# Gate splits at other ticks, decay work ordered behind retention scores, other statistics for three last tiles and a later silu table in a one-core encoder layer

## Chip, cores and metric

The kernel runs on one core of a Trainium2 chip. The metric is the device time of one execution in microseconds (us): the median of three runs of the kernel before is 1171.52 us, from 1171.24 to 1172.17.

## What is computed

One layer of an encoder on 1024 tokens of width 1024, all in float32. In the words of the reference, cut:

```python
u = x @ w_in                                        # rq rk rv rg | aq ak av
y_ret = swish(rg) * groupnorm(ret_fwd + ret_bwd)    # 8 heads of 64, chunks of 128
y_att = windowed_gqa(aq, ak, av, sink)              # 8 query heads, 2 kv heads, +-128 tokens, ALiBi
h = layer_norm(ALPHA * x + concat(y_ret, y_att) @ w_out)
ffn = (silu(h @ w_gate) * (h @ w_up)) @ w_down      # hidden 2816
ple = sigmoid(h @ w_ple_gate) * (p @ w_ple_proj)
out = layer_norm(ALPHA * h + ffn + ple)
```

Retention of one direction and one head is done in 8 chunks: `scores = q @ k.T * decay`, `y_inner = scores @ v`, `kv = (k * k_decay).T @ v` of each chunk, a scan `state = state * chunk_decay + kv` over the chunks, and `y_cross = (q * q_decay) @ state`.

## The kernel before

Every large float32 matmul is three fp32r passes: an operand is split into a high part (ScalarE copy) and a low part (VectorE subtraction, lines 71 and 72), and TensorE adds hi*hi, hi*lo and lo*hi (lines 77 to 79 in the first phase, 803 to 805 later). The products with W_out, with w_ple_gate and of the feed-forward part are made by a seven-product scheme (Strassen's), so their operands are first added or subtracted in halves.

**The order of the first phase, to about 355 us.** TensorE's order is written out by hand, as a list of steps ("ticks", some 0.9 us each). Eight heads of retention and eight of attention are done in four pairs. While one pair's retention and attention are worked on, TensorE multiplies the next pair's projections, step by step, and small pieces of the pair's own work are put between these steps. VectorE, ScalarE, SyncE (SP, which issues the DMAs) and GpSimd (POOL) get their order from a scheduler, which places their instructions beside TensorE's; `behind` is an order dependency without a semaphore that keeps an instruction behind the latest matmul of the main stream. The retention pieces of one pair are, in class `Retention`: `keys` (transposes of k into PSUM, then VectorE's multiplication by the key decay, line 411; the tiles are called `qq` for chunks 0 to 3 and `pt` for 4 to 7), `kv` (matmuls at line 428 out of both tiles, evicted by VectorE at 436 and by ScalarE at 434), `scan` (12 small instructions at 441 and 444, then four DMAs that write the states), `scores` (matmuls at 459, multiplication by the decay at 461 into `pt`, and the queries' decay at 464 into `qq`), `out` (matmuls at 478 to 481), `evict` (ScalarE squares at 488 and 489, VectorE at 490 and 491) and `norm` (matmuls with ones at 498, then 500, and 519 some ticks later). Attention's pieces are `scores` (548 and 549, with VectorE's bias and maximum at 550, `st` at 552, ScalarE's exponential at 554; some ticks later 558 and the scaling at 560), `turn` (transposes at 572, evicted at 574) and `values` (584).

**Side work.** The weight w_ple_gate is split ahead of its use: `presplit_gate` makes 28 operands. Each is one `put` (ScalarE copy at 602, VectorE subtraction at 603, one 512 KB store to DRAM tensor `pgd` by SP), 16 of them behind one VectorE sum at 663. They rotate through two buffers `pro`. The list `at` gives the tick at which each of 30 items is put out. Line 251 is the eviction of attention's queries (`aq`).

**W_out.** About 354 to 376 us VectorE makes sums and low halves of W_out's operands (lines 870, 872, 876 and 72), ScalarE the high halves (71) and evictions of the first products (972).

**Feed-forward.** From about 541 us all five engines' orders are written by hand. Units of 12 matmul passes (2.72 us each) make gate and up products; `finish` applies ScalarE's Silu in place (1388). A one-element Silu stands ahead of the units in the code (1854); the table of an activation function is loaded by an ACT_TABLE_LOAD ahead of the first instruction that needs another table.

**The end.** The last unit finishes tiles 0 to 3 of the output one after the other, 18 matmul passes each, in `tail`: add the product (`addto`, 1618 or 1620), mean and variance (`var`), reciprocal deviation (`rstd`: VectorE, then POOL's power at 1652), `center` (1657, times the gain) and `scale` (1662, plus the bias, then a 256 KB store of each half on SP). For tile 3 the statistics come from VectorE's bn_stats and bn_aggr (1622, 1641); for tiles 0 to 2 the sum comes with the addition (1618) or from ScalarE (1624), and the squares from ScalarE (1635). Tiles 4 to 7 are finished earlier by `ln2_steps`: ScalarE at 1674, VectorE at 1677, and a DMA issued from POOL that adds the bias to the tile (1678), then one 512 KB store each on SP.

Of the kernel before, what the change touches and what calls it, by code (L numbers as in the profile page):

```python
# [16 lines left out]
P = 128  # L17
# [25 lines left out]
def layer(tc, xT, xn, w_first, w_mt, w_rv, w_out, w_pg, w_pe, pT, w_gu, w_dn,  # L43
# [37 lines left out]
    def behind(ins):  # L81

        tc.add_manual_dep(ins.ins, recent[0], mybir.DependencyInfo(
            mybir.DependencyClass.NoSync, mybir.DependencyReason.DATA), reason="order")
        return ins
# [307 lines left out]
    class Retention:  # L393
# [44 lines left out]
        def scan(self):  # L438
            i, U = self.i, self.U
            for n in range(1, 7):  # L440
                dve.scalar_tensor_tensor(U[0][:, n, :], U[0][:, n - 1, :], cd[:, i:i + 1], U[0][:, n, :],
                                         ALU.mult, ALU.add)
                k = 6 - n
                dve.scalar_tensor_tensor(U[1][:, k, :], U[1][:, k + 1, :], cd[:, 4 + i:5 + i], U[1][:, k, :],
                                         ALU.mult, ALU.add)
# [4 lines left out]
        def scores(self, hh):  # L450
# [9 lines left out]
            for h in range(2):  # L460
                dve.tensor_tensor(pt[:, h], bb[h], self.dt[:, h, :].unsqueeze(1).to_broadcast([P, 4, P]), ALU.mult)
            qq = self.qq[hh] = bt([P, 2, 4, P], "qq")
            for h in range(2):
                dve.tensor_tensor(qq[:, h], dq[:, h, :].rearrange("p (n c) -> p n c", n=4),
                                  self.qd[:, h, :].unsqueeze(1).to_broadcast([P, 4, P]), ALU.mult)
# [179 lines left out]
    def presplit_gate():  # L645
# [9 lines left out]
        def steps(k):  # L655
# [21 lines left out]
        at = [2 + 3.4 * k for k in range(12)] + [55 + 2.5 * k for k in range(2)] + [65 + 1.9 * k for k in range(7)] + \  # L677
            [78.5 + 2 * k for k in range(9)]
# [935 lines left out]
    def addto(t, h, b, op=ALU.add, done=False):  # L1614


        if done and t != LAST and op == ALU.add:
            dve.tensor_tensor_reduce(half(t, h), half(t, h), b, 1.0, 0.0, op, ALU.add, stts[t][:, h:h + 1])
            return
        dve.tensor_tensor(half(t, h), half(t, h), b, op)  # L1620
        if done and t == LAST:
# [4 lines left out]
    LAST = 3  # L1626
# [10 lines left out]
    def var(t):  # L1637

        stt = stts[t]
        if t == LAST:  # L1640
# [6 lines left out]
    def rstd(t):  # L1647
        stt = stts[t]
        if t != LAST:
# [32 lines left out]
    def tail(products):  # L1682

        bs = dbank[len(SEG) - 1, GRP[4]]
        for t in range(4):
            products(t)
            if t:
                rstd(t - 1)
            addto(t, 0, bs[t], done=True)
            var(t)  # L1690
            if t < LAST:
                if t:
                    scale(t - 1)
                center(t)
        rstd(LAST)
        scale(LAST - 1)
        center(LAST)
        scale(LAST)
# [140 lines left out]
    with tc.manual_schedule(engines={ET.PE, ET.DVE, ET.Activation, ET.Pool, ET.SP}):  # L1839
# [14 lines left out]
        act.activation(fsum[3][:, 0:1], fsum[0][:, 0:1], AF.Silu)  # L1854
        ahead_g(-1, 4)
        for k in range(NG):
# [9 lines left out]
            ahead_g(k, k + 1 + min(9, 4 + k))  # L1866
            while stores and stores[0][0] <= k:
# [105 lines left out]
```

## Time and profile before

| | before |
|---|---|
| median of 3 runs | 1171.52 us |
| the profiled execution's own time | 1172.7 us |
| span of its trace | 1170.6 us |
| granted clock of TensorE | 0.998 |
| TensorE (PE) busy | 1156.5 us, 99% |
| VectorE (DVE) busy | 900.4 us, 77% |
| ScalarE (ACT) busy | 580.1 us, 50% |
| GpSimd (POOL) busy | 121.0 us, 10% |
| SP's DMA queue | 195.94 MB, 47.6% of 16 DMA engines' span |
| POOL's DMA queue | 16.78 MB, 8.2% |

A row of a timeline gives the start, the busy time, the engine, the line of the kernel, the operation, the tile written and the tiles read, their shape, a count where several alike follow one another, and in brackets the idle time before it with what ended that. Instructions of one engine overlap somewhat: one of 0.69 us can follow the last by 0.60.

### The profile page before, as it was taken

To read this page: it belongs to the slowest core of one execution; us is meant where nothing else is said; L and a number is where in the kernel's file an instruction comes from. 1 tells how busy PE (TensorE), PEld (TensorE's weight loads), DVE (VectorE), ACT (ScalarE), POOL (GpSimd) and SP (SyncE) were. 2 spreads that over 40 slices of the span, in tenths; PEclk is the share of its full clock that TensorE was granted. 3 is DMA by queue.
4 is the path that set the end of the run, shared out by engine and by line. 5 is a ranking of instruction groups with operands and counts; after the bars stand their busy time and mean duration, and the time that the engine had idled before them with its cause. 6 is when DMAs were issued, how large, how long until landed. Compare 5 with 4: busy or idle time off the path is not lost.

```text
span 1170.6 us, 17933 instructions
## 1 busy us (share of the span) xinstructions
PE 1156.5 (99%) x6330; PEld 971.5 (83%) x6330; DVE 900.4 (77%) x1746; ACT 580.1 (50%) x1181; POOL 121.0 (10%) x181
## 2 busy tenths in 40 slices
PE   9999999999999999999999999999999999999996
PEld 7888888788887888888888888888888888888885
DVE  4666688777869688947998988888888976773677
ACT  5566348686756256214445434443344445552463
POOL 2001021202010021000000000000000020133232
PEclk9999999999999999999999999999999999999999
DMA  6345665746356955665322222232223289999977
GB/s 252 100 153 207 246 207 193 244 159 223 127 190 230 365 172 196 261 195 201 117 90 105 112 105 100 102 135 101 99 72 136 89 249 349 350 225 203 261 173 216
DMA packets 84378, 213.86 MB, mean 183 GB/s; under 512 B 12225, under 2 KB 17473, under 8 KB 84289
## 3 DMA queue, kind: packets, MB, share of 16 engines
q1 hardware_dynamic: 75648, 195.94, 47.6%
q0 software_dynamic: 8640, 16.78, 8.2%
q8 instruction: 50, 0.82, 0.3%
q14 instruction: 40, 0.32, 0.1%
HBM read 141.32 MB, written 62.16 MB: 174 GB/s over the span
## 4 chain that ended last, share of the span: by engine, by line
PE 86%; DVE 6%; DMA 4%; ACT 2%; issue 1%; POOL 0%; SPq 0%; DVEq 0%; ACTq 0%; POOLq 0%
PE bmm L803 8%; PE bmm L804 8%; PE bmm L805 7%; PE bt L803 6%; PE bt L804 6%; PE bt L805 6%; PE bmm L77 4%; PE bs L803 4%; PE bs L805 4%; PE bs L804 4%; PE bmm L79 4%; PE bmm L78 4%; PE bo L805 3%; PE bo L803 3%; PE bo L804 3%
## 5 line engine op out<-in xcount | busy, mean ns | idle before, releaser
L77 PE MATMUL bmm<-H,w 128*128 128x512 f32 x240 | 97.3, 405 | 0.0
L78 PE MATMUL bmm<-H,w 128*128 128x512 f32 x240 | 93.9, 391 | 0.0
L79 PE MATMUL bmm<-H,w 128*128 128x512 f32 x240 | 93.9, 391 | 0.0
L1388 ACT ACTIVATE ev<-ev 128x512 f32<-128x512 f32 x42 | 26.5, 630 | 104.3 <-DVE ev L1417 92.8
L1562 POOL DMA_DIRECT2D h0b<-in_w_dn x24 | 21.6, 899 | 540.7 <-DVE ev L1368 504.9
L77 PEld LDWEIGHTS bmm<-H,w 128*128 128x128 f32 x240 | 45.1, 188 | 11.1 <-issue 1.4
L79 PEld LDWEIGHTS bmm<-H,w 128*128 128x128 f32 x240 | 45.1, 188 | 10.3
L78 PEld LDWEIGHTS bmm<-H,w 128*128 128x128 f32 x240 | 45.2, 188 | 7.9
L554 ACT ACTIVATE sc<-sc,st 128x385 f32<-128x385 f32 (+1 forms) x64 | 37.2, 585 | 15.6 <-DVE st L552 15.3
L550 DVE CUSTOM_DVE_ANT_0 sc<-cst,bs,skb 128x384 f32<-128x384 f32 (+1 forms) x64 | 35.0, 575 | 8.3 <-PE bs L549 7.8
L1417 DVE TENSOR_TENSOR ev<-ev,bt 128x512 f32<-128x512 f32 x44 | 30.1, 683 | 12.5 <-PE bt L805 12.5
L1368 DVE TENSOR_TENSOR ev<-ev,bs 128x256 f32<-128x256 f32 x63 | 25.6, 418 | 15.5 <-PE bs L805 14.7
L1390 DVE TENSOR_TENSOR ev<-ev 128x512 f32<-128x512 f32 x42 | 29.0, 691 | 10.5 <-ACT ev L1388 9.0
L803 PE MATMUL bmm<-H,u 128*128 128x512 f32 x92 | 36.2, 393 | 0.2 <-ACT ev L1426 0.2
L804 PE MATMUL bmm<-H,u 128*128 128x512 f32 x92 | 36.0, 392 | 0.0
L805 PE MATMUL bmm<-H,u 128*128 128x512 f32 x92 | 35.8, 389 | 0.0
L72 DVE TENSOR_TENSOR w<-raw,w 128x512 fp32r<-128x512 f32 x34 | 23.1, 688 | 16.2 <-ACT w L71 16.1
L545 POOL COPY sc<-skb 128x1 f32<-128x1 f32 x64 | 15.6, 253 | 188.9 <-PE bt L572 144.5
L560 ACT ACTIVATE sc<-sc,st 128x384 f32<-128x384 f32 (+1 forms) x64 | 34.2, 580 | 1.2 <-DVE st L558 0.9
L71 ACT ACTIVATE H<-ln 128x512 fp32r<-128x512 f32 (+1 forms) x34 | 22.7, 675 | 21.2 <-DVE ln L1052 7.2
L803 PE MATMUL bmm<-H,w 128*128 128x512 f32 x84 | 32.9, 392 | 0.0
L804 PE MATMUL bmm<-H,w 128*128 128x512 f32 x84 | 32.9, 392 | 0.0
(802 smaller groups left out, 3898.4 us busy)
## 6 DMA issues: line engine op xcount, KB each, us to landing
ad<-ev SPq DMA_DIRECT2D x33, 512.0 KB, 2.6
pgd<-pro SPq DMA_DIRECT2D x28, 512.0 KB, 3.0
raw<-in_w_gu SPq DMA_DIRECT2D x22, 512.0 KB, 3.6
ln<-in_w_gu SPq DMA_DIRECT2D x22, 512.0 KB, 3.9
raw<-ad SPq DMA_DIRECT2D x40, 256.0 KB, 5.6
ln<-ad SPq DMA_DIRECT2D x37, 256.0 KB, 6.0
H<-in_w_dn SPq DMA_DIRECT2D x33, 256.0 KB, 7.4
wod<-aq SPq DMA_DIRECT2D x15, 512.0 KB, 2.8
```

Source lines behind the costliest of these rows:

```text
L77: pe.matmul(o, lh, rh, start=start, stop=False)
L78: pe.matmul(o, lh, rl, start=False, stop=False)
L79: recent[0] = pe.matmul(o, ll, rh, start=False, stop=stop).ins.name
L550: dve.tensor_tensor_reduce(sc[g][:, :nk], cst[:, tc0:tc0 + nk], b[:, :nk], slope(i, g), skb[:, 2 * i + g:2 * i + g + 1], ALU.add, ALU.max, ...
L554: act.activation(sc[g][:, :nk + 1], sc[g][:, :nk + 1], AF.Exp, bias=st_[:, 1, j, g:g + 1], accum_out=st_[:, 2, j, g:g + 1])
L560: behind(act.activation(sc[g][:, :nk], sc[g][:, :nk], AF.Copy, scale=st_[:, 3, j, g:g + 1]))
L803: pe.matmul(o, lh, rh, start=start, stop=False, skip_group_check=True)
L804: pe.matmul(o, lh, rl, start=False, stop=False, skip_group_check=True)
L805: pe.matmul(o, ll, rh, start=False, stop=stop, skip_group_check=True)
L1388: act.activation(c[:, 0, :], c[:, 0, :], AF.Silu)
L1390: dve.tensor_tensor(c[:, 1, :], c[:, 0, :], c[:, 1, :], ALU.mult)
L1417: dve.tensor_tensor(get(name), ev[left][:, m, :], right, ALU.add)
```

## The change

Four places change. (1) The list `at`, which spreads the gate's 30 split items over ticks: the first 14 follow one another by 2.8 ticks in place of 12 by 3.4 and 2 from tick 55 by 2.5; the next 7 begin at tick 60 in place of 65, the last 9 at 73 by 1.9 in place of 78.5 by 2. (2) A new order dependency `after`, without a semaphore, puts the 12 scan instructions and the two multiplications by the queries' decay behind the second multiplication of the retention scores (`pt`) on VectorE. (3) At the end, tiles 1 and 2 get their statistics from bn_stats and bn_aggr as tile 3 does; tile 0 is scaled by one ScalarE instruction, its bias is added by a DMA from POOL, and one 512 KB store writes it; `scale` of a tile follows its `center` at once. (4) The one-element Silu moves behind the first feed-forward unit.

```diff
--- before.py
+++ after.py
@@ -81,6 +81,11 @@
     def behind(ins):
 
         tc.add_manual_dep(ins.ins, recent[0], mybir.DependencyInfo(
+            mybir.DependencyClass.NoSync, mybir.DependencyReason.DATA), reason="order")
+        return ins
+
+    def after(ins, name):
+        tc.add_manual_dep(ins.ins, name, mybir.DependencyInfo(
             mybir.DependencyClass.NoSync, mybir.DependencyReason.DATA), reason="order")
         return ins
 
@@ -438,11 +443,12 @@
         def scan(self):
             i, U = self.i, self.U
             for n in range(1, 7):
-                dve.scalar_tensor_tensor(U[0][:, n, :], U[0][:, n - 1, :], cd[:, i:i + 1], U[0][:, n, :],
-                                         ALU.mult, ALU.add)
                 k = 6 - n
-                dve.scalar_tensor_tensor(U[1][:, k, :], U[1][:, k + 1, :], cd[:, 4 + i:5 + i], U[1][:, k, :],
-                                         ALU.mult, ALU.add)
+                for x in (dve.scalar_tensor_tensor(U[0][:, n, :], U[0][:, n - 1, :], cd[:, i:i + 1], U[0][:, n, :],
+                                                   ALU.mult, ALU.add),
+                          dve.scalar_tensor_tensor(U[1][:, k, :], U[1][:, k + 1, :], cd[:, 4 + i:5 + i], U[1][:, k, :],
+                                                   ALU.mult, ALU.add)):
+                    after(x, self.tail)
             for d in range(2):
                 for h in range(2):
                     sp.dma_start(self.states[64 * d:64 * d + 64, h, 1 - d:NT - d, :], U[d][64 * h:64 * h + 64])
@@ -458,11 +464,12 @@
                     a = slice(64 * h, 64 * h + 64)
                     pe.matmul(bb[h][:, j, :], self.rk[a, c], dq[a, h, j * P:(j + 1) * P], start=True, stop=True)
             for h in range(2):
-                dve.tensor_tensor(pt[:, h], bb[h], self.dt[:, h, :].unsqueeze(1).to_broadcast([P, 4, P]), ALU.mult)
+                self.tail = dve.tensor_tensor(pt[:, h], bb[h], self.dt[:, h, :].unsqueeze(1).to_broadcast([P, 4, P]),
+                                              ALU.mult).ins.name
             qq = self.qq[hh] = bt([P, 2, 4, P], "qq")
             for h in range(2):
-                dve.tensor_tensor(qq[:, h], dq[:, h, :].rearrange("p (n c) -> p n c", n=4),
-                                  self.qd[:, h, :].unsqueeze(1).to_broadcast([P, 4, P]), ALU.mult)
+                after(dve.tensor_tensor(qq[:, h], dq[:, h, :].rearrange("p (n c) -> p n c", n=4),
+                                        self.qd[:, h, :].unsqueeze(1).to_broadcast([P, 4, P]), ALU.mult), self.tail)
 
         def half(self, hh):
             return self.y[:, hh * HF:(hh + 1) * HF]
@@ -674,8 +681,7 @@
         k0, k1, k2, k3 = map(steps, range(4))
         k1[0] = pair_of(k1[0], lambda: load(2))
         k3[0:0] = [lambda: load(3), lambda: None]
-        at = [2 + 3.4 * k for k in range(12)] + [55 + 2.5 * k for k in range(2)] + [65 + 1.9 * k for k in range(7)] + \
-            [78.5 + 2 * k for k in range(9)]
+        at = [2 + 2.8 * k for k in range(14)] + [60 + 1.9 * k for k in range(7)] + [73 + 1.9 * k for k in range(9)]
         return [(ticks[0] + t, f) for t, f in zip(at, k0 + k1 + k2 + k3, strict=True)]
 
     def pair_of(f, g):
@@ -1614,16 +1620,16 @@
     def addto(t, h, b, op=ALU.add, done=False):
 
 
-        if done and t != LAST and op == ALU.add:
+        if done and t not in BN and op == ALU.add:
             dve.tensor_tensor_reduce(half(t, h), half(t, h), b, 1.0, 0.0, op, ALU.add, stts[t][:, h:h + 1])
             return
         dve.tensor_tensor(half(t, h), half(t, h), b, op)
-        if done and t == LAST:
+        if done and t in BN:
             dve.bn_stats(stts[t][:, 6 * h:6 * h + 6], half(t, h))
         elif done:
             act.activation(ct([P, HF], "sg", 2), half(t, h), AF.Copy, accum_out=stts[t][:, h:h + 1])
 
-    LAST = 3
+    BN = (1, 2, 3)
 
     def negmean(t):
         stt = stts[t]
@@ -1637,7 +1643,7 @@
     def var(t):
 
         stt = stts[t]
-        if t == LAST:
+        if t in BN:
             dve.bn_aggr(stt[:, 12:14], stt[:, 0:12])
             dve.tensor_scalar(stt[:, 12:13], stt[:, 12:13], -1.0, None, ALU.mult)
         else:
@@ -1646,7 +1652,7 @@
 
     def rstd(t):
         stt = stts[t]
-        if t != LAST:
+        if t not in BN:
             dve.tensor_scalar(stt[:, 13:14], stt[:, 2:3], stt[:, 3:4], 1.0 / D, ALU.add, ALU.mult)
         dve.tensor_scalar(stt[:, 14:15], stt[:, 13:14], EPS, None, ALU.add)
         pool.tensor_tensor(stt[:, 15:16], stt[:, 14:15], cst[:, C_MH:C_MH + 1], ALU.pow)
@@ -1684,18 +1690,20 @@
         bs = dbank[len(SEG) - 1, GRP[4]]
         for t in range(4):
             products(t)
-            if t:
-                rstd(t - 1)
+            if t == 1:
+                rstd(0)
             addto(t, 0, bs[t], done=True)
             var(t)
-            if t < LAST:
-                if t:
-                    scale(t - 1)
-                center(t)
-        rstd(LAST)
-        scale(LAST - 1)
-        center(LAST)
-        scale(LAST)
+            if t in BN:
+                rstd(t)
+            if t == 1:
+                act.activation(accd[0], accd[0], AF.Copy, scale=stts[0][:, 15:16])
+                pool.dma_start(accd[0], ln2[1], accum_op=ALU.add)
+            center(t)
+            if t in BN:
+                scale(t)
+            if t == 1:
+                sp.dma_start(out[0], accd[0])
 
     GRP = {1: 0, 2: 0, 5: 1, 3: 1, 6: 2, 7: 2, 4: 2}
 
@@ -1851,7 +1859,6 @@
         homes.update((name, a_tile([P, 2, HF], "ev")) for name in ("spare", "s1", "u2", "c11", "u3", "c22"))
         FINE4 = len(plan(0)) + len(plan(1)) - 2
         FINES = (2, 4, 7, 9, 20, 23, 26, FINE4)
-        act.activation(fsum[3][:, 0:1], fsum[0][:, 0:1], AF.Silu)
         ahead_g(-1, 4)
         for k in range(NG):
             gunits[k][1]()
@@ -1864,6 +1871,8 @@
                     items.insert(at, x)
                     at += 1
             ahead_g(k, k + 1 + min(9, 4 + k))
+            if k == 0:
+                act.activation(fsum[3][:, 0:1], fsum[0][:, 0:1], AF.Silu)
             while stores and stores[0][0] <= k:
                 stores.pop(0)[1]()
             j = k + 1 - NG
```

TensorE's order is the same in both kernels. Three places of VectorE's order follow, in the lines of each kernel (411, 603, 663 and 251 before are 416, 610, 670 and 256 after).

VectorE at the start of pair 1, before: the last rows up to the key decay of chunks 4 to 7 (`pt` at 411), which TensorE's first kv matmuls read; `aq` is evicted out of two PSUM banks, and ScalarE has a part of each eviction.

```order
L251 SCALAR_TENSOR_TENSOR aq_466<-bmm_1470,aq_466 64x512
L603 TENSOR_TENSOR pro_1168<-pre_1165,pro_1168 128x512
L251 SCALAR_TENSOR_TENSOR aq_1548<-bmm_1470,aq_1548 64x512
L72 TENSOR_TENSOR w_1608<-raw_1606,w_1608 128x512
L500 TENSOR_SCALAR kv_1592<-bo_1516 2x512
L251 SCALAR_TENSOR_TENSOR aq_466<-bmm_1558,aq_466 64x512
L411 TENSOR_TENSOR qq_1603<-bt_1598,kd 128x512 x2
L251 SCALAR_TENSOR_TENSOR aq_1548<-bmm_1558,aq_1548 64x512
L72 TENSOR_TENSOR w_1611<-raw_1606,w_1611 128x512
L411 TENSOR_TENSOR pt_1632<-bt_1627,kd 128x512 x2
L519 SCALAR_TENSOR_TENSOR y_1162<-y_1162,gn,kv_1485 128x512
```

The same place after the change.

```order
L256 SCALAR_TENSOR_TENSOR aq_466<-bmm_1477,aq_466 64x512
L256 SCALAR_TENSOR_TENSOR aq_1560<-bmm_1477,aq_1560 64x512
L610 TENSOR_TENSOR pro_1167<-pre_1165,pro_1167 128x512
L72 TENSOR_TENSOR w_1616<-raw_1614,w_1616 128x512
L610 TENSOR_TENSOR pro_1168<-pre_1166,pro_1168 128x512
L256 SCALAR_TENSOR_TENSOR aq_466<-bmm_1566,aq_466 64x512
L507 TENSOR_SCALAR kv_1600<-bo_1528 2x512
L416 TENSOR_TENSOR qq_1611<-bt_1606,kd 128x512
L256 SCALAR_TENSOR_TENSOR aq_1560<-bmm_1566,aq_1560 64x512
L416 TENSOR_TENSOR qq_1611<-bt_1606,kd 128x512
L72 TENSOR_TENSOR w_1619<-raw_1614,w_1619 128x512
L416 TENSOR_TENSOR pt_1640<-bt_1635,kd 128x512 x2
```

Two operands of the gate (610) stand here in place of one, two instructions of 416 are parted by an eviction, and the normalization of the last pair (519 before) no longer follows the key decay directly.

VectorE at the start of pair 2, before: the rows up to the same key decay.

```order
L603 TENSOR_TENSOR pro_1168<-pre_1163,pro_1168 128x512
L663 TENSOR_TENSOR pre_1164<-pre_1164,pre_1163 128x512
L519 SCALAR_TENSOR_TENSOR y_1596<-y_1596,gn,kv_2110 128x512
L251 SCALAR_TENSOR_TENSOR aq_2236<-bmm_2242,aq_2236 64x512
L411 TENSOR_TENSOR qq_2330<-bt_2325,kd 128x512
L603 TENSOR_TENSOR pro_1167<-pre_1163,pro_1167 128x512
L251 SCALAR_TENSOR_TENSOR aq_2237<-bmm_2242,aq_2237 64x512
L411 TENSOR_TENSOR qq_2330<-bt_2325,kd 128x512
L603 TENSOR_TENSOR pro_1168<-pre_1164,pro_1168 128x512
L72 TENSOR_TENSOR w_2335<-raw_2333,w_2335 128x512
L72 TENSOR_TENSOR w_2338<-raw_2333,w_2338 128x512
L411 TENSOR_TENSOR pt_2360<-bt_2355,kd 128x512 x2
```

And after.

```order
L256 SCALAR_TENSOR_TENSOR aq_2249<-bmm_2125,aq_2249 64x512
L507 TENSOR_SCALAR kv_2288<-bo_2201 2x512
L72 TENSOR_TENSOR w_2335<-raw_2333,w_2335 128x512
L610 TENSOR_TENSOR pro_1168<-pre_1164,pro_1168 128x512
L526 SCALAR_TENSOR_TENSOR y_1604<-y_1604,gn,kv_2116 128x512
L256 SCALAR_TENSOR_TENSOR aq_2248<-bmm_2254,aq_2248 64x512
L416 TENSOR_TENSOR qq_2330<-bt_2325,kd 128x512 x2
L256 SCALAR_TENSOR_TENSOR aq_2249<-bmm_2254,aq_2249 64x512
L72 TENSOR_TENSOR w_2338<-raw_2333,w_2338 128x512
L416 TENSOR_TENSOR pt_2360<-bt_2355,kd 128x512 x2
```

Counted from the eviction of the pair's last output (490 before, 497 after) to the second multiplication into `pt`, VectorE has 23 instructions before and 18 after: five splits and sums of the gate have moved ahead of it.

VectorE at the start of W_out, before, from the last sums of line 870 to the second of line 876 (`ln`, `h0a`, `H` and `h` are operands of W_out's products).

```order
L870 TENSOR_TENSOR ln_3854<-y_1597,y_2323 128x512
L72 TENSOR_TENSOR H_3852<-ln_3853,H_3852 128x512 x2
L872 TENSOR_TENSOR ln_3854<-ln_3854,y_1596 128x512
L72 TENSOR_TENSOR H_3851<-ln_3854,H_3851 128x512
L876 TENSOR_TENSOR ln_3853<-ln_3853,y_2321 128x512
L72 TENSOR_TENSOR H_3852<-ln_3854,H_3852 128x512
L872 TENSOR_TENSOR ln_3854<-ln_3854,y_1597 128x512
L72 TENSOR_TENSOR h0a_3895<-ln_3853,h0a_3895 128x512
L72 TENSOR_TENSOR h_3897<-y_2321,h_3897 128x512
L72 TENSOR_TENSOR H_3852<-ln_3854,H_3852 128x512
L876 TENSOR_TENSOR ln_3853<-ln_3853,y_2322 128x512
```

And after (876, 878 and 882 are 870, 872 and 876 before).

```order
L878 TENSOR_TENSOR ln_3854<-ln_3854,y_1604 128x512
L876 TENSOR_TENSOR ln_3854<-y_1605,y_2323 128x512
L882 TENSOR_TENSOR ln_3853<-ln_3853,y_2321 128x512
L72 TENSOR_TENSOR H_3852<-ln_3854,H_3852 128x512
L72 TENSOR_TENSOR H_3851<-ln_3854,H_3851 128x512
L72 TENSOR_TENSOR h0a_3895<-ln_3853,h0a_3895 128x512
L878 TENSOR_TENSOR ln_3854<-ln_3854,y_1605 128x512
L72 TENSOR_TENSOR h_3897<-y_2321,h_3897 128x512
L882 TENSOR_TENSOR ln_3853<-ln_3853,y_2322 128x512
```

From the first instruction of line 870 to the second of line 876 VectorE has 20 instructions before and 19 after. On ScalarE the table load and the one-element Silu that stood in this stretch are gone; the load that stood right in front of the first Silu of line 1388 now stands earlier, between a split (1252) and an eviction (1424) of the first units. The program has 6 table loads before and 5 after.

## The prediction

> **What bounds the kernel now.** First the busy times of the page, then TensorE's waits, then the last of the stretches into which I cut the span (its second number is TensorE's busy time).
>
> ```profile
> PE 1156.5 (99%) x6330; PEld 971.5 (83%) x6330; DVE 900.4 (77%) x1746; ACT 580.1 (50%) x1181; POOL 121.0 (10%) x181
> ...
> PE bt L428 <- DVE pt L411: 2.0, 1, 2.0
> PE bs L803 <- ACT h0b L972: 0.6, 1, 0.6
> ...
> PE bt L572 <- ACT ptr L574: 0.3, 1, 0.3
> PE bmm L803 <- ACT ev L1426: 0.2, 1, 0.2
> ...
> 1162.00:1170.60 8.60, 0.00 (x0) 0.00 (x0) 5.57 (x11) 0.00 (x0) 1.22 (x2) 0.76 0.42 161
> ```
>
> TensorE is busy 1156.5 of 1170.6 us, and its order stays. So the change can gain only where TensorE stands still, 14.1 us: 8.6 of them after its last matmul, the others in waits of which one is 2 us long and the rest are under 1. What parts 1, 2 and 4 can bring is therefore small, and what they can spoil is larger: VectorE works three quarters of the time right beside TensorE.
>
> **Pair 2's start: a gain.** VectorE ahead of the long wait, and TensorE's kv matmuls in pair 1 and in pair 2:
>
> ```profile
> 228.92 0.68 DVE L603 TENSOR_TENSOR pro<-pre,pro 128x512 fp32r<-128x512 f32 x1
> 229.52 1.29 DVE L72 TENSOR_TENSOR w<-raw,w 128x512 fp32r<-128x512 f32 x2
> 230.73 1.28 DVE L411 TENSOR_TENSOR pt<-bt,kd 128x512 f32<-128x512 f32 x2
> ...
> 169.33 1.03 PE L428 MATMUL bt<-rv,qq 128*64 128x64 f32 x28
> 170.19 0.99 PE L428 MATMUL bt<-rv,pt 128*64 128x64 f32 x28
> ...
> 229.16 1.03 PE L428 MATMUL bt<-rv,qq 128*64 128x64 f32 x28
> 232.16 0.53 PE L428 MATMUL bt<-rv,pt 128*64 128x64 f32 x11 [1.97 <-DVE pt L411]
> ```
>
> The second 28 matmuls begin 0.86 us behind the first in pair 1, 3.00 behind in pair 2: 2.14 lost, as the key decay ended only at 230.73 + 1.28 = 232.01. Back to back, VectorE starts such instructions 0.60 apart (228.92, 229.52). After the change 18 instead of 23 stand from the pair's last eviction to the decay's end, which so moves 5 x 0.60 = 3.0 us ahead, to 229.0; TensorE wants it at 229.16 + 0.86 = 230.02. **-2.15**, with 1 us of slack, enough for one late instruction. Late next is nothing near: the scan, now behind the scores' `pt`, is read several ticks later.
>
> A smaller stall is that of the turn in pair 1:
>
> ```profile
> 181.17 0.39 PE L79 MATMUL bmm<-H,w 128*128 128x512 f32 x1
> 181.84 0.33 PE L572 MATMUL bt<-cst,sc 128*128 128x128 f32 x1 [0.28 <-ACT ptr L574]
> ```
>
> Passes follow one another by 0.227; here 0.67 pass. ScalarE's scaling ahead of it hangs on a VectorE reciprocal, which now has fewer scan and split instructions before it: **-0.45**, between that and 0.
>
> **Pairs 0 and 1: losses.** The splits moved ahead must stand somewhere. In pair 1 there is little room:
>
> ```profile
> 160.25 0.69 DVE L490 COPY y<-bo 128x512 f32<-128x512 f32 x1 [2.95 <-ACT pt L489]
> ...
> 168.62 1.29 DVE L411 TENSOR_TENSOR pt<-bt,kd 128x512 f32<-128x512 f32 x2
> ...
> 165.88 0.59 ACT L250 ACTIVATE aq<-bmm 64x512 fp32r<-64x512 f32 x1 [1.21 <-DVE aq L251]
> ```
>
> The decay ended at 169.91 and TensorE took it at 170.19 without a wait: slack under 0.3. Between the eviction at 160.25 and the decay's end 15 instructions stand in place of 14, one gate operand more, 0.60 to 0.72. VectorE's 2.95 us of idle time lie ahead of this stretch, so they do not cover it; and in it `aq` goes to and fro between VectorE and ScalarE (the 1.21), so a delay can count twice. The decay then ends at 170.6 to 171.3: a stall of 0.5 to 1.2, bounds 0 and 1.4. I take **+0.9**, as both engines are nearly full there. Behind it, attention's next scores need both banks that `pt` of the retention scores frees, and that stands behind a normalization, two copies and a reciprocal which waits for ScalarE's exponential: **+0.4**, bounds 0 and 1.0, nearer to the low end as only one bank is late. In pair 0 the low half of the squares gets a gate operand and a sum ahead of it:
>
> ```profile
> 149.74 0.68 DVE L491 TENSOR_TENSOR rb<-kv,kv 128x512 fp32r<-128x512 f32 x1
> ...
> 151.40 0.39 PE L498 MATMUL bo<-rb,ones 128*128 128x512 f32 x1
> ```
>
> It ended at 150.42, 1.0 ahead of TensorE. Two multiplications of `qq` go from before it, two gate instructions come, and each gate operand may wait for the store out of its buffer: **+0.2**, bounds 0 and 0.4. The pairs together: -2.15 - 0.45 + 0.9 + 0.4 + 0.2 = **-1.1**, by the bounds from -2.6 to +0.7.
>
> **W_out's start: a small gain.** ScalarE, then VectorE, at the wait for h0b:
>
> ```profile
> 362.84 1.28 ACT L1854 ACT_TABLE_LOAD   x1
> ...
> 371.90 0.63 ACT L71 ACTIVATE h0a<-ln 128x512 fp32r<-128x512 f32 x1 [1.78 <-DVE ln L876]
> 372.44 0.58 ACT L972 ACTIVATE h0b<-bs 128x512 f32<-128x512 f32 x1
> ...
> 371.19 0.68 DVE L876 TENSOR_TENSOR ln<-ln,y 128x512 f32<-128x512 f32 x1
> ```
>
> TensorE waits for the eviction at 372.44; it stands behind the split at 371.90, and that behind VectorE's 371.19, before which ScalarE idles 1.78. So the load taken out at 362.84 brings nothing by itself: ScalarE is not late there. But the scheduler has placed the second 876 one instruction sooner, 19th in place of 20th: **-0.6**, bounds -0.6 (the whole wait) and 0.
>
> **Silu's table: a small gain.** ScalarE, then TensorE:
>
> ```profile
> 549.79 1.28 ACT L1388 ACT_TABLE_LOAD   x1 [2.41 <-DVE ev L1417]
> 557.46 0.58 ACT L1426 ACTIVATE ev<-bmm 128x512 f32<-128x512 f32 x1
> ...
> 557.50 0.39 PE L805 MATMUL bmm<-H,w 128*128 128x512 f32 x1
> 558.09 0.50 PE L803 MATMUL bmm<-H,u 128*128 128x512 f32 x1 [0.20 <-ACT ev L1426]
> ```
>
> The table had been replaced before the first Silu, so it came again, 1.28 us in ScalarE's chain. Moved ahead, it lies in the 2.41 us that ScalarE idled, and the stall of 0.59 - 0.227 goes: **-0.35**, bounds -0.36 and 0. Were that cover too short, the load would delay the eviction next to it, and the price would be of the same size.
>
> **The end: about nothing.** Tile 0's and tile 1's additions, tile 3's chain, and the DMAs of the last 35 us:
>
> ```profile
> 1149.56 0.69 DVE L1618 CUSTOM_DVE_ANT_0 acc<-acc,bmm 128x512 f32<-128x512 f32 x1 [0.40 <-PE bmm L805]
> ...
> 1153.64 0.69 DVE L1618 CUSTOM_DVE_ANT_0 acc<-acc,bmm 128x512 f32<-128x512 f32 x1 [0.35 <-PE bmm L805]
> ...
> 1161.80 0.69 DVE L1620 TENSOR_TENSOR acc<-acc,bs 128x512 f32<-128x512 f32 x1 [0.18 <-PE bs L805]
> 1162.52 0.69 DVE L1622 BATCH_NORM_STATS2 stt<-acc 128x6 f32<-128x512 f32 x1
> 1163.25 0.21 DVE L1641 BATCH_NORM_AGGREGATE stt<-stt 128x2 f32<-128x12 f32 x1
> ...
> 1163.62 1.40 DVE L1662 SCALAR_TENSOR_TENSOR acc<-acc,stt,u 128x512 f32<-128x512 f32 x2
> 1164.94 1.41 DVE L1657 SCALAR_TENSOR_TENSOR acc<-acc,stt,u 128x512 f32<-128x512 f32 x2
> 1166.27 1.41 DVE L1662 SCALAR_TENSOR_TENSOR acc<-acc,stt,u 128x512 f32<-128x512 f32 x2
> ...
> acc<-u POOLq DMA_DIRECT2D x4, 512.0 KB, 4.9
> out_y<-acc SPq DMA_DIRECT2D x4, 512.0 KB, 3.6
> ```
>
> Before, tile 2's scale (1163.62, 1.32 start to start) still stands in tile 3's chain; after, each tile is finished by itself: 0.72 + 0.73 + 0.37 + 1.32 + 1.33 = 4.47 us by the starts above, while TensorE makes a tile in 1153.64 - 1149.56 = 4.08. Two more bn_stats (2 x 0.60) ahead of tile 0 meet 0.40 of idle time: tile 0 starts 0.8 late, tile 1, 3.7 behind it without its idle 0.35, at 1154.1. Then tile 2 begins at 1158.6, tile 3 at 1163.0, and the last scale ends at 1167.5 in place of 1167.68: 1.3 saved, 1.2 lost, **-0.1**, bounds -0.6 and +0.5. Tile 0 leaves by another way: scaled on ScalarE at about 1156, its bias added by a DMA that POOL issues at about 1157, behind tile 1's power; at 4.9 us it lands at 1162, and SP's store, 3.6, ends at 1165.5. Tile 2's halves, ready at 1162.3 and 1163, stand behind it on SP, then tile 3's at 1167. What this costs the last store by sharing: **+0.2**, bounds 0 and +2.
>
> **A rule against the change.** POOL's issue beside a busy VectorE:
>
> ```profile
> 1146.81 2.34 DVE L1677 TENSOR_TENSOR acc<-acc,u 128x1024 f32<-128x1024 f32 x2
> 1148.43 0.89 POOL L1678 DMA_DIRECT2D acc<-u  x1 [2.57 <-DVE acc L1677]
> ```
>
> It took 0.89 us although VectorE was at work for most of them, so VectorE's additions did not hold it up. The Trainium skill, "SBUF — State Buffer", section "SBUF: two separate sides", warns that a DMA issued from GpSimd needs its cores to write descriptors, and that some modes of VectorE lock them out; under "Who interferes with whom" it infers that two-input operations do not. The row agrees with the second. Were the issue held until VectorE is done at 1167.5, tile 0's bias would land at 1172.4 and its store end at 1176, 6.3 us after the last landing of before (about 1169.7): by the lock the sum would be near +4.5, about 1176.
>
> **Sum.** -1.1 - 0.6 - 0.35 - 0.1 + 0.2 = -1.95. The profiled execution took 1172.7 (span 1170.6, so 2.1 lie around it); its like would take 1170.7. The median of the three runs is 1171.52, 1.2 lower: **1169.5 us**. A measurement of this kernel can tell about 0.2%, 2.3 us, from no change.
>
> **Rivals.**
> - *No new stall in pairs 0 and 1*: the scheduler's order fits TensorE after all; the +1.5 falls away: -3.45, 1168.1, down to 1167.2 with the end at its low bound. For it: ScalarE and VectorE both have idle time just ahead. Against it: 0.28 of slack at 170.19. Chance 0.22.
> - *The stall only moves*: the to and fro of `aq` counts twice, and the losses stand at their bounds, 1.4 + 1.0 + 0.4, against -2.6; with W_out and Silu at half (-0.5) and the end at +0.1: about -0.2, 1171.3; own range 1170.5 to 1172.3. Chance 0.20.
> - *Slower, at the end*: tile 0's bias DMA lands late, as POOL's four of line 1678 (median 4.9) are each queued behind the last, and SP's later stores stand behind tile 0's. It decides from a landing at 1167, when tile 3's first half is ready, ten us after the issue; from there each us is one at the end. At 1169: store and halves share 3.6 us and more, the end 3 us late, sum +1 to +4, 1172.5 to 1175.5. For it: the order on SP. Against it: twice the median. Chance 0.08, the lock above included.
> - *It does not do what it says*: `pro` has two buffers, so an operand put out earlier can wait for a store, and all runs in the old times: about 1171. Chance 0.04.
>
> The forecast has 0.46; its own range is 1168.2 to 1170.6. The range of all is 1167.3 to 1172.3; outside are the slower rival and a few hundredths of the first. Faster by over 0.2%: the first rival and four tenths of the forecast, 0.40; slower, the third and a little of the second, 0.10; within, 0.50.
>
> **What would show it.** Right: no wait of the kv matmuls at 230, one of 0.5 to 1.2 at about 170; no table load at 362, and ScalarE's first Silu without one; tile 3's addition 1.0 to 1.4 behind TensorE's end, and tile 0's store landed before tile 3's. Wrong: a wait above 1.4 in pairs 0 or 1, a last scale more than 6.5 us behind TensorE's end (5.9 before), or tile 0's store issued after tile 2 is ready by more than 3 us.

## The result, and the profile after

The changed kernel takes 1173.24 us (median of 20 runs, 1170.10 to 1174.85) against 1171.15 of the kernel before in as many runs beside it (1169.81 to 1173.66): a ratio of 1.0013, 95% interval 1.0007 to 1.0019. That is about 1.5 us slower by the ratio (2.1 by the medians), where 2 us faster was forecast, and it lies above the range. The profiled execution took 1173.84, with a span of 1172.0 against 1170.6. The profiled execution of before (1172.7) was itself 1.5 us over its median, so the two spans differ by less than the medians.

TensorE's first pass of W_out starts at 357.38 in place of 354.63: up to there 2.75 us are lost. From there to the start of its last pass it takes 805.38 in place of 806.74: behind the pairs 1.36 us are gained. The loss lies in the pairs.

TensorE's waits in the changed kernel:

```profile
PE bs L555 <- DVE pt L467: 1.8, 1, 1.8
PE bo L147 <- POOL sq L144: 1.3, 1, 1.3
PE bt L809 <- ACT h0b L978: 1.1, 1, 1.1
PE bt L433 <- DVE pt L416: 0.8, 1, 0.8
PE bt L579 <- ACT ptr L581: 0.4, 1, 0.4
PE bt L809 <- DMA u<-wod: 0.2, 1, 0.2
PE bo L505 <- DVE rb L498: 0.2, 1, 0.2
```

The wait of 2.0 for the key decay is down to 0.8, and it is another one: it stands in pair 1 now. On top stands a wait that was not in the list of before: attention's scores (line 555) for the second multiplication by the retention decay (467). Pair 2's start is free, and Silu's table lies in idle time:

```profile
233.83 0.98 PE L433 MATMUL bt<-rv,qq 128*64 128x64 f32 x28
234.68 0.82 PE L433 MATMUL bt<-rv,pt 128*64 128x64 f32 x21
...
546.61 0.63 ACT L1258 ACTIVATE w<-sums 128x512 fp32r<-128x512 f32 x1 [2.36 <-DVE sums L1294]
547.26 1.28 ACT L1875 ACT_TABLE_LOAD   x1
```

The two groups of kv matmuls begin 0.85 us apart, as in pair 1 before (0.86), where before the change 3.00 lay between them. And no wait of the first feed-forward units is left.

Pair 1 tells the rest. SP's queue, then VectorE, then TensorE, in the changed kernel:

```profile
166.53 0.41 SPq L518 DMA_DIRECT2D rnd<-sn  x1
170.19 0.33 SPq L116 DMA_DIRECT2D raw<-in_w_mt  x1
170.63 1.10 SPq L522 DMA_DIRECT2D kv<-rnd  x2
...
169.45 0.68 DVE L72 TENSOR_TENSOR w<-raw,w 128x512 fp32r<-128x512 f32 x1
...
173.70 0.69 DVE L467 TENSOR_TENSOR pt<-bs,dt 128x512 f32<-128x512 f32 x1
175.99 0.75 DVE L526 SCALAR_TENSOR_TENSOR y<-y,gn,kv 128x512 f32<-128x512 f32 x1 [1.60 <-DMA kv<-rnd]
176.66 0.68 DVE L441 COPY kv<-bt 128x256 f32<-128x256 f32 x2
177.26 0.68 DVE L467 TENSOR_TENSOR pt<-bs,dt 128x512 f32<-128x512 f32 x1
...
175.88 0.34 PE L556 MATMUL bs<-kz,aq 128*128 128x384 f32 x1
178.00 0.44 PE L555 MATMUL bs<-k,aq 128*128 128x384 f32 x1 [1.78 <-DVE pt L467]
178.52 0.63 PE L77 MATMUL bmm<-H,w 128*128 128x512 f32 x1
178.95 0.63 PE L78 MATMUL bmm<-H,w 128*128 128x512 f32 x1
```

Read it from below. TensorE waits at 176 for a PSUM bank that the second `pt` at 177.26 frees. Ahead of that stands the normalization of pair 0 (526), and VectorE idles 1.60 us for its reciprocals, which two DMAs of line 522 fetch. These were issued only at 170.63, as the load ahead of them on SP (116) waits until VectorE has read the old contents of its buffer (72, done at 170.13). A wait of one engine for a buffer has held up a DMA of another chain behind it in the same queue. Behind the stall the passes follow one another by 0.43 in place of 0.227 us. The stretches show why; the column before the last two is the granted clock:

```profile
170.00:178.00 8.00, 5.46 (x81) 4.46 (x76) 5.16 (x15) 3.49 (x10) 1.63 (x1) 1.00 0.34 101
178.00:182.00 4.00, 4.00 (x11) 3.29 (x12) 3.48 (x11) 1.59 (x5) 0.24 (x1) 0.57 0.16 42
```

From 178 to 182 the clock was 0.57: 0.43 x 4 = 1.7 us more in this execution.

The same place before the change, SP's queue and TensorE's scores:

```profile
163.43 0.38 SPq L511 DMA_DIRECT2D rnd<-sn  x1
165.79 1.10 SPq L515 DMA_DIRECT2D kv<-rnd  x2
...
168.66 0.34 SPq L111 DMA_DIRECT2D raw<-in_w_mt  x1
...
174.86 0.34 PE L549 MATMUL bs<-kz,aq 128*128 128x384 f32 x1
175.03 0.36 PE L548 MATMUL bs<-k,aq 128*128 128x384 f32 x1
```

The fetch went out 2.36 us behind its store and ahead of the load, and the scores followed one another without a wait.

W_out's start, before and then in the changed kernel, and the end of the program in the changed kernel:

```profile
353.06 0.75 DVE L519 SCALAR_TENSOR_TENSOR y<-y,gn,rb 128x512 f32<-128x512 f32 x1 [1.62 <-DMA rb<-rnd]
...
353.49 0.69 DVE L730 SCALAR_TENSOR_TENSOR y<-sq,y 128x512 f32<-128x512 f32 x1
355.40 0.75 DVE L526 SCALAR_TENSOR_TENSOR y<-y,gn,rb 128x512 f32<-128x512 f32 x1 [1.21 <-DMA rb<-rnd]
356.07 3.69 DVE L72 TENSOR_TENSOR H<-y,H 128x512 fp32r<-128x512 f32 x6
...
1158.03 0.90 POOL L1701 DMA_DIRECT2D acc<-u  x1
1164.04 0.33 SPq L1706 DMA_DIRECT2D out_y<-acc  x1
...
1162.76 0.39 PE L811 MATMUL bs<-u,u 128*128 128x512 f32 x1
1164.10 0.68 DVE L1626 TENSOR_TENSOR acc<-acc,bs 128x512 f32<-128x512 f32 x1
1167.31 1.41 DVE L1668 SCALAR_TENSOR_TENSOR acc<-acc,stt,u 128x512 f32<-128x512 f32 x2
```

VectorE's full stretch at W_out begins in both kernels with a normalization that waits for a fetch; it comes 2.3 us later, while TensorE itself comes 2.75 later. The end hangs on TensorE as before: from its last pass (1162.76) to the end of the span 9.24 us, before 1170.6 - 1161.37 = 9.23.

### The profile page after: what moved, and what is told of

Read it like the earlier page. It is cut to its first block, busy times and chain, and to the rows that moved or that the text cites. A ratio compares the mean times of both kernels' runs of the same rounds, so it can differ in the third digit from the quotient of the medians.

```text
span 1172.0 us, 17919 instructions
## 1 busy us (share of the span) xinstructions
PE 1157.2 (99%) x6330; PEld 972.9 (83%) x6330; DVE 902.5 (77%) x1746; ACT 577.1 (49%) x1169; POOL 127.6 (11%) x182
## 4 chain that ended last, share of the span: by engine, by line
PE 90%; DVE 4%; DMA 2%; ACT 2%; issue 1%; SPq 0%; POOL 0%; DVEq 0%; ACTq 0%
PE bmm L809 8%; PE bmm L810 8%; PE bmm L811 8%; PE bt L809 6%; PE bt L810 6%; PE bt L811 6%; PE bmm L77 5%; PE bmm L78 5%; PE bmm L79 5%; PE bs L811 4%; PE bs L810 4%; PE bs L809 4%; PE bo L811 4%; PE bo L810 4%; PE bo L809 4%; PE bo L591 2%
## 5 line engine op out<-in xcount | busy, mean ns | idle before, releaser
L77 PE MATMUL bmm<-H,w 128*128 128x512 f32 x240 | 97.7, 407 | 0.1
L78 PE MATMUL bmm<-H,w 128*128 128x512 f32 x240 | 94.5, 394 | 0.0
L79 PE MATMUL bmm<-H,w 128*128 128x512 f32 x240 | 94.4, 393 | 0.0
L809 PE MATMUL bmm<-H,w 128*128 128x512 f32 x84 | 32.9, 392 | 0.0
L810 PE MATMUL bmm<-H,w 128*128 128x512 f32 x84 | 32.9, 392 | 0.0
L811 PE MATMUL bmm<-H,w 128*128 128x512 f32 x84 | 32.7, 389 | 0.0
```

What stands on the lines that cost most here:

```text
L77: pe.matmul(o, lh, rh, start=start, stop=False)
L78: pe.matmul(o, lh, rl, start=False, stop=False)
L79: recent[0] = pe.matmul(o, ll, rh, start=False, stop=stop).ins.name
L809: pe.matmul(o, lh, rh, start=start, stop=False, skip_group_check=True)
L810: pe.matmul(o, lh, rl, start=False, stop=False, skip_group_check=True)
L811: pe.matmul(o, ll, rh, start=False, stop=stop, skip_group_check=True)
```

## The experiments

All comparisons are with the kernel before on the same chip; intervals are 95%. Edits are against the changed kernel unless it is said otherwise. The theory to start with (A): the gate's new ticks hold up pair 0's normalization on SP. The rivals: the order dependency does it (B), or the new end (C).

**The old ticks** (parts 2, 3 and 4 stay):

```diff
-        at = [2 + 2.8 * k for k in range(14)] + [60 + 1.9 * k for k in range(7)] + [73 + 1.9 * k for k in range(9)]
+        at = [2 + 3.4 * k for k in range(12)] + [55 + 2.5 * k for k in range(2)] + [65 + 1.9 * k for k in range(7)] + \
+            [78.5 + 2 * k for k in range(9)]
```

> The changed kernel with the gate's old ticks (parts 2, 3, 4 stay). Theory A, the gate's new ticks hold up pair 0's normalization on SP, so that TensorE loses 1.9 us in attention's scores of pair 1 and some 1.7 more in a slow clock behind it: both stalls of pair 1 and the slow matmuls of 178 to 181 are gone, the wait of 2 us at pair 2's start is back (or part of it), the time is 0.5 to 1.5 us under the kernel before, about 1170. Theory B, the order dependency of part 2 puts the second multiplication by the retention decay too late: the stall at attention's second scores stays at 1 us or more and the time is over the kernel before by 1 us or more. Theory C, the new tail costs it: 1 to 1.5 us over the kernel before with no stall in pair 1.

Measured: ratio 1.0003 (0.9990 to 1.0016). No stall in pair 1; 1.4 and 0.5 us at pair 2's start, and 1.8 us at W_out. The stalls of pair 1 follow A, but the time is no gain over the kernel before.

**The new ticks alone**: the kernel before with the new list, the diff above the other way round.

> The kernel before with the gate's new ticks alone. Theory A: the stalls of pair 1 appear (about 1 us at the kv matmuls, 1.5 or more at attention's second scores) and the clock may drop behind them; pair 2's wait is smaller; 1 to 2.5 us over the kernel before. Theory B: no stall above 0.5 us at attention's second scores, and a gain of 1 us or more. Theory C: a gain as in B.

Measured: 0.9994 (0.9985 to 1.0003), where A expected a loss. TensorE's waits in pairs 1 and 2 are short:

```profile
PE bt L579 <- ACT ptr L581: 0.3, 1, 0.3
PE bs L555 <- DVE pt L467: 0.2, 1, 0.2
```

The scores' wait is 0.2 in place of 1.8, and no wait of line 433 is left, in pair 1 or 2. So A falls: the ticks alone remove pair 2's wait and bring nothing like it in pair 1. The gain of 1 us or more that B and C had is not there either: 0.7 us, not clear of zero.

**The old end** (parts 1, 2 and 4 stay):

```diff
-    BN = (1, 2, 3)
+    LAST = 3
+    BN = (3,)
...
-            if t == 1:
-                rstd(0)
+            if t:
+                rstd(t - 1)
...
-            if t in BN:
-                scale(t)
-            if t == 1:
-                sp.dma_start(out[0], accd[0])
+            if t < LAST:
+                if t:
+                    scale(t - 1)
+                center(t)
...
```

> The changed kernel with the end of before (parts 1, 2, 4 stay). Theories A and B: the pair 1 stalls as in the changed kernel, and the time from TensorE's last matmul to the end within 0.5 us of the changed kernel's 8.9, so the time within 0.6 us of the changed kernel's. Theory C: 1 us or more faster than the changed kernel.

Measured: 1.0012 (1.0002 to 1.0022), like the changed kernel. C falls: between the two ends no difference shows that is clear of the noise. The stalls of pair 1 are there as in the changed kernel (0.7 and 1.7), but in this profile the clock behind them is not down:

```profile
178.00:182.00 4.00, 4.00 (x22) 3.43 (x21) 3.95 (x16) 2.16 (x7) 0.59 (x2) 1.00 0.35 98
```

**The end and Silu's place alone**: the kernel before with parts 3 and 4.

> The kernel before with parts 3 and 4 alone (the end and Silu's table). By the sum of the prediction: Silu 0.36 gained at the 557 us stall, W_out 0 to 0.6, the end within 0.3: 0.3 to 0.9 us under the kernel before in all theories but C, which has it 0.5 us or more over.

Measured: 0.9994 (0.9984 to 1.0004), 0.7 us, in the range of the sum but not clear of zero.

What was left was the dependency, or its meeting with the ticks (A2).

**Without the dependency** (parts 1, 3 and 4):

```diff
-                    after(x, self.tail)
+                    pass
...
-                after(dve.tensor_tensor(qq[:, h], dq[:, h, :].rearrange("p (n c) -> p n c", n=4),
-                                        self.qd[:, h, :].unsqueeze(1).to_broadcast([P, 4, P]), ALU.mult), self.tail)
+                dve.tensor_tensor(qq[:, h], dq[:, h, :].rearrange("p (n c) -> p n c", n=4),
+                                  self.qd[:, h, :].unsqueeze(1).to_broadcast([P, 4, P]), ALU.mult)
```

> The changed kernel without the order dependency of part 2 (parts 1, 3, 4 stay). Theory A2: only the new ticks and the order dependency together part the two multiplications by the retention decay and put the late normalization between them; then the stalls of pair 1 stay under 0.5 us each, pair 2's wait stays away, and the time is 1 to 1.6 us under the kernel before, the sum of the gains that parts 1 and 3 with 4 showed alone (0.7 each). Rival B2: the end and the gate's ticks together cost it, whatever the order; then the time stays within 0.7 us of the changed kernel's and above the kernel before.

Measured: 0.9999 (0.9990 to 1.0007), 1.6 us under the changed kernel by the ratios, but not the 1 to 1.6 under the kernel before that A2 had. Pair 1 has no wait. The 1.1 of lines 555 and 467 is now that of pair 2, at 233.4, where the queries' decay stands ahead of `pt`:

```profile
PE bt L809 <- ACT h0b L978: 1.2, 1, 1.2
PE bs L555 <- DVE pt L467: 1.1, 1, 1.1
```

So B2 falls, and A2 holds for pair 1. Pair 2 shows what the dependency is good for.

**The normalization later**: it goes out 6 ticks later, and so stands behind both `pt` on VectorE; SP's order is unchanged.

```diff
-            later.extend((ticks[0] + at, f) for at, f in zip(LAGS, (spread, power, store, fetch, scaled)))
+            lags = LAGS[:-1] + (LAGS[-1] + (6 if (self.i, hh) == (0, 0) else 0),)
+            later.extend((ticks[0] + at, f) for at, f in zip(lags, (spread, power, store, fetch, scaled)))
```

> The changed kernel with the normalization of pair 0's first half put out 6 ticks later, so that VectorE's order has it behind both multiplications by the retention decay; SP's order is that of the changed kernel, with the load still ahead of the fetch. Theory A2 with the place on VectorE as cause: the stall at attention's second scores falls from 1.9 to under 0.3 us, the slow matmuls behind it are gone, 2 to 4 us under the changed kernel. Rival: the stall is set by the reciprocal of attention's maximum and ScalarE ahead of it; then 0.5 us or more of it stays.

Measured: 1.0004 (0.9995 to 1.0012), about 1 us under the changed kernel, where 2 to 4 were expected. The stall at the scores is gone, but half of it comes back at the turn behind, for another reader of SP's queue:

```profile
173.98 1.29 DVE L467 TENSOR_TENSOR pt<-bs,dt 128x512 f32<-128x512 f32 x2
176.81 0.69 DVE L441 COPY kv<-bt 128x256 f32<-128x256 f32 x2 [1.54 <-DMA sn<-kv]
...
179.78 0.71 PE L580 MATMUL bt<-cst,sc 128*128 128x128 f32 x4 [0.84 <-ACT kv L439]
```

The eviction of the kv matmuls needs a buffer that the next DMA on SP (`sn`) still reads, and that one stands behind the same load and fetch.

**The load behind the fetch** on SP; VectorE's order is unchanged.

```diff
-    recent = [None]
+    recent, got, nload = [None], [None], [0]
...
-        sp.dma_start(r, src)
+        x = sp.dma_start(r, src)
+        nload[0] += 1
+        if got[0] and nload[0] == 11:
+            after(x, got[0])
...
-                    sp.dma_start(r[64 * h:64 * h + 64], home[64 * h:64 * h + 64].rearrange("q e -> (q e)").partition_broadcast(64))
+                    got[0] = sp.dma_start(r[64 * h:64 * h + 64], home[64 * h:64 * h + 64].rearrange("q e -> (q e)").partition_broadcast(64)).ins.name
```

> The changed kernel with one load of a projection's weight on SP moved behind the fetch of the normalization's reciprocals; VectorE's order is that of the changed kernel. If the load, which waits for its buffer until 170.1, is what makes the fetch late: the fetch is issued about 1.7 us sooner, VectorE's wait of 1.6 us for it is gone or under 0.3, the stall falls from 1.9 to about 0.3 to 0.6; 1.3 to 3 us under the changed kernel. Rival: the fetch is late by its own chain (the store of the gate's operands ahead of it); then the stall falls by under 0.7.

Measured: 1.0008 (0.9998 to 1.0018). SP and VectorE:

```profile
167.27 0.41 SPq L521 DMA_DIRECT2D rnd<-sn  x1
169.69 1.10 SPq L525 DMA_DIRECT2D kv<-rnd  x2
...
174.23 0.17 DVE L568 RECIPROCAL st<-st 128x2 f32<-128x2 f32 x1 [1.16 <-ACT sc L564]
174.32 0.75 DVE L529 SCALAR_TENSOR_TENSOR y<-y,gn,kv 128x512 f32<-128x512 f32 x1
```

The fetch goes 2.4 us behind the store in place of 4.1, VectorE waits for it no more, and the list of TensorE's waits has no scores in it, although the normalization and the copies still stand ahead of the second `pt`. The fetches of this line also land sooner, 2.8 us after their issue in place of 4.4 (medians of two). So the load was the cause of that wait. The time shows little of it: 0.6 us under the changed kernel by the ratios, where 1.3 to 3 were expected, and not clear of the noise. In this profile, which lies 1.7 us over the median of its runs, W_out's wait is 2.0, again with a slow clock behind it (0.57 from 368 to 372).

**Both edits together.**

> Both edits, the later normalization and the load behind the fetch, in the changed kernel. Theory A2: as the better one of the two alone, since both take away the same wait; no stall above 0.3 at attention's second scores, 2 to 4 us under the changed kernel, 1 to 2 us under the kernel before. If the two waits were independent, it would gain the sum of both.

Measured: 1.0005 (0.9997 to 1.0014). No stall at the scores; 0.8 at pair 1's key decay, 0.5 at a turn and 1.8 at W_out are left. They take away the same wait, as expected, but 1 us or more under the kernel before was wrong: about 0.9 us under the changed kernel is all that is left of it.

**The last normalization left out** (that half of the last head pair's retention output stays unscaled), to see what starts VectorE's stretch at W_out:

```diff
+                if (self.i, hh) == (3, 1):
+                    return
                 behind(dve.scalar_tensor_tensor(y, y, gn[:, self.i:self.i + 1], r, ALU.mult, ALU.mult))
```

> The changed kernel without the last normalization's multiplication (second half of pair 3; that part of the retention output stays unscaled). Nothing else of the order moves but its neighbours. If VectorE's full stretch at W_out is released by the fetch of that normalization: it begins 1 to 4 us sooner, and the waits of 1.65 us in all at W_out fall under 0.5; 1 to 1.6 us under the changed kernel. Rival (my prediction's reading, the stretch is bound by VectorE's own order): the waits stay above 1.2 us.

Measured: 0.9998 (0.9988 to 1.0008), 1.8 us under the changed kernel by the ratios. VectorE's timeline:

```profile
351.66 0.69 DVE L732 SCALAR_TENSOR_TENSOR y<-sq,y 128x512 f32<-128x512 f32 x1
352.33 4.30 DVE L72 TENSOR_TENSOR H<-y,H 128x512 fp32r<-128x512 f32 x7
```

And TensorE's waits, but for the start:

```profile
PE bs L557 <- DVE pt L467: 1.7, 1, 1.7
PE bt L433 <- DVE pt L416: 0.8, 1, 0.8
...
```

The stretch begins 0.67 us behind the row ahead of it, in place of 2.58 (353.49 to 356.07 in the changed kernel), and the wait for h0b is gone. So VectorE is late at W_out since it starts late, by a DMA, and not only since it is full; of the 1.9 us, some 0.7 are the normalization's own time.

**The dependency in pair 2 alone**, and **in pairs 2 and 3**:

```diff
+                    if self.i >= 2:
-                    after(x, self.tail)
+                        after(x, self.tail)
...
+                if self.i >= 2:
+                    after(x, self.tail)
```

(with `== 2` in the first of the two, and `x` for the multiplication by the queries' decay in the lower place)

> The changed kernel with the order dependency in pair 2 alone. In the profile without it TensorE lost 1.3 us in pair 2 at attention's second scores, behind the multiplication by the queries' decay, and nothing in pair 1. Theory A2 (the dependency does harm in pair 1, where the late normalization gets between, and good in pair 2): no stall above 0.3 us at attention's second scores in either pair, 1 to 1.5 us under the kernel without the dependency, so 1 to 2 us under the kernel before. Rival (what TensorE gains before W_out is taken back there, since VectorE's stretch begins with a DMA): the stall goes but W_out's grows by about as much, and the time stays within 0.4 us of 1171.

> As the run before, with the order dependency in pairs 2 and 3. If the dependency in pair 3 moves the last normalization's DMAs on SP and so the start of VectorE's stretch at W_out: 0.3 to 1 us slower than with pair 2 alone, with the difference at the W_out waits of 355 to 372. Rival: pair 3 has slack, the two agree within 0.3 us.

Measured: 0.9990 (0.9981 to 0.9999) and 0.9982 (0.9973 to 0.9991), medians 1170.31 and 1169.98 against 1171.24. Neither has a stall at the scores in pair 1 or 2. The second, TensorE's waits but for the start:

```profile
PE bt L812 <- DMA w<-wod: 0.9, 1, 0.9
PE bt L812 <- ACT h0b L981: 0.5, 1, 0.5
PE bt L582 <- ACT ptr L584: 0.3, 1, 0.3
PE bt L812 <- DMA u<-wod: 0.3, 1, 0.3
```

It is the fastest version here, some 2.1 us under the kernel before and 3.6 under the changed one by the ratios. It differs from the changed kernel by the dependency of pairs 0 and 1 alone, so there lies the harm; the waits that went are those of pair 1, and 0.2 in pair 0. The dependency does no harm in pair 3; whether it helps there, the two intervals don't tell.

**The dependency alone**, in the kernel before:

> The kernel before with the order dependency of part 2 alone. Theory A2: with the old ticks the two multiplications by the retention decay stay together in pair 1 and no normalization comes between; no new stall in pair 1, the wait of 2 us at pair 2's start stays; W_out's waits may grow by up to 1 us as in the run with the old ticks: 0 to 1 us over the kernel before. Rival: the dependency alone brings the stall of pair 1; then 1.5 us or more over.

Measured: 1.0010 (1.0001 to 1.0020). No stall in pair 1, pair 2's start as before (1.4 and 0.8 of waits). By the ratio it costs about 1.2 us with the old ticks too, a little more than expected, and its profile does not show where: its span is 1170.9 against 1170.6, and the profiled execution of before lay 1.5 us over its median.

## Why the prediction was wrong

| term | predicted | in the changed kernel's profile |
|---|---|---|
| pair 2's start | -2.15 | 0.85 apart in place of 3.00: -2.15 |
| pair 1's key decay | +0.9 | starts 1.79 apart in place of 0.86: +0.9 |
| attention's next scores | +0.4, at most 1.0 | 2.12 apart in place of 0.17: +1.9 |
| the clock behind it | not in the sum | +1.7 in this execution |
| pair 0's squares | +0.2 | wait of 0.2 |
| the turn | -0.45 | gone at 181, one of 0.4 at a later turn (211) |
| W_out's start | -0.6 | passes lose 1.84 over their spacing in place of 2.18: -0.3 |
| Silu's table | -0.35 | passes 0.23 apart in place of 0.59: -0.36 |
| the end | +0.1 | 0.0 |

The last column adds up to about +1.9; the spans differ by 1.4. Of the rest 0.4 lies ahead of all these places: at 100 us the changed kernel's passes stand 0.37 sooner.

**The step that failed** is the one on attention's next scores: "a normalization, two copies and a reciprocal which waits for ScalarE's exponential: +0.4, bounds 0 and 1.0". The place and the instructions were right; the price was taken from the instructions' own time. The normalization waits for a DMA, and that DMA's queue on SP was not followed, where the load that waits for VectorE had come ahead of the fetch. The step counts VectorE's rows and none of SP's. The runs showed 1.9 in its place: the run with the load moved had the same instructions ahead of the scores, and no wait. The prediction's own sign of being wrong, a wait above 1.4 in pair 1, came.

**W_out's start came half right.** "The scheduler has placed the second 876 one instruction sooner" was so, and the wait named there is gone; but TensorE now waits 1.1 us for another eviction into `h0b`, sooner in its order, and over the whole stretch 0.3 us is gained in place of 0.6, within the bounds. What the step did not see is that VectorE's full stretch begins when the last normalization's fetch lands: without that normalization the passes lose 0.5 us there. In the other profiles the wait for `h0b` goes from 0.3 to 2.0 us, so a saving in the pairs can be given back there, as in the profile with both edits.

**Right size, wrong cause**: pair 1's key decay. The prediction laid its 0.9 to the gate's earlier ticks. With the ticks alone, and with all but the dependency, that wait is gone, so the agreement is luck. It comes when dependency and ticks meet: in VectorE's rows of the changed kernel the first two evictions `aq` follow one another without a gate operand between them, and VectorE idles 0.66 us for ScalarE there.

**Pair 2's start** was right in size and cause: with the ticks alone the wait at 230 is gone, with the dependency alone it stays. One reading was wrong without harm: beside the wait of 2.0 "the rest are under 1", but TensorE's list of before has one of 1.3 (line 142 for POOL), the same in every run.

**The rivals.** The second, the stall that only moves, was the nearest, and still too low: it had the losses of instructions, and no price for the fetch. The slower rival at the end did not come: tile 0's bias was issued at 1158.03 and its store at 1164.04, 2 us later than said, ahead of 1167. That VectorE's work holds up POOL's DMA shows in neither kernel: tile 0's issue took 0.90 us while VectorE's two-input instructions ran from 1156.91 to 1159.65.

**The slow clock is not what the median lost.** The granted clock of each run is on record: its mean is 0.9973 over the 20 runs of the changed kernel and 0.9974 to 0.9975 over the three groups of runs of the kernel before beside the experiments. Four us at 0.57 in each would take 0.43 x 4 / 1172 = 0.0015 off; 0.0002 is 0.2 us. The nine runs of the changed kernel at 0.998 took 1173.2 us in the mean, those of the kernel before at 0.998 1171.3 to 1171.4.

What stays open: how the loss of the median divides. By the ratios it goes with the dependency: 1.6 us with the new ticks, 1.2 with the old, and 3.6 between the changed kernel and the one that has it in pairs 2 and 3 alone. How much of it is the wait at the scores is not shown, as the two runs that remove this wait by the load's place gain 0.6 and 0.9 us, not clear of the noise. Where the dependency alone loses its microsecond is not known. Parts do not add up to the whole: ticks alone 0.9994, end and Silu 0.9994, both 0.9999.

## What to carry to other kernels

Where a DMA stands in the chain that a waiting instruction needs, follow its queue too: write down the transfers ahead of it and what each of them waits for, since a load that waits for a buffer holds all that stand behind it. An order dependency that helps at one place of a loop can do harm at another; put it only where a profile shows the wait, here in pair 2. And before a gain is booked ahead of a stretch in which another engine is full, look what starts that stretch.

## What the runs showed of the hardware

A stall of some 2 us of TensorE can be followed by 3 to 4 us at a granted clock of 0.57, with passes 0.43 us apart in place of 0.227. In the 14 profiles here it came twice: behind the 1.9 us of the changed kernel's profile and behind the 2.0 us at W_out in the run with the load moved, but not behind the same stall with the old end, nor behind the 1.97 us of the kernel before. The Trainium skill, "TensorE: Matmul & The Clock Gate", section "What's actually happening", has the clock halved after an idle window of about 3.4 us that runs freely; its section "Wait — 56ns, not 53.3ns?" gives 426.7 ns as the spacing of such passes at the halved clock. The spacing agrees, and that it comes in one execution and not in another fits a free window. But here 1.8 us of waiting, with another 0.8 some 5 us before, was enough, and in the other profile a single wait of 1.96 us.

DMAs of SP's queue went out in their order: a load that waited for its buffer until 170.13 was issued at 170.19, and the fetch behind it at 170.63, 4.1 us after its store; with the load behind it, the fetch went out after 2.4.
